# The first RMSNorm of a hybrid decoder step: its squares summed on VectorE alone, its products earlier in TensorE's order

## Chip, cores and metric

The kernel runs on one core of a Trainium2 chip. The metric is the device time in microseconds of one execution. Several executions are timed and the median is given; one further execution is recorded by the hardware profiler, and all rows of "the profile" come from that one.

The engines are called as in the profile: PE (TensorE; PEld are its weight loads), DVE (VectorE), ACT (ScalarE), POOL (GpSimd) and SP (SyncE, which here only issues DMA transfers). Each engine takes its instructions in the order of its own queue.

## What is computed

The reference is one inference step of a decoder layer: a group of 1024 prompt tokens and a group of 8 x 4 sample tokens share the weights. Cut to what matters here:

```python
def rmsnorm(x, g):
    var = jnp.mean(x * x, axis=-1, keepdims=True)
    return x * lax.rsqrt(var + EPS) * g

def reference(x_prompt, x_sample, mem_prompt, ..., norm_mix, w_in, ..., w_mem_k, w_mem_v, ...):
    p_mem_k = einsum('bmd,lde->lbme', mem_prompt, w_mem_k)      # (256 memory rows, 1024) @ (1024, 1024)
    p_mem_v = einsum('bmd,lde->lbme', mem_prompt, w_mem_v)
    ...
    u = rmsnorm(h, norm_mix)                                    # h is x at first
    proj = einsum('bld,de->ble', u, w_in)
    ...                                                         # mixers, cross-attention, SwiGLU, final norm
```

Everything is float32. Each float32 operand of a matrix product is split into a high and a low part (`hi`, `lo`), and three products hi*hi, hi*lo and lo*hi are summed, so each product costs three matmuls and each operand one ACT copy (the high part) and one subtraction on DVE or POOL (the low part).

## The kernel before

Activations lie feature by token: `x` is 8 tiles of 128 features by T = 1056 tokens (1024 prompt, 32 sample). The kernel begins with a stage that does two things side by side.

*The memory keys and values.* There are 16 weight strips `w_kv[i]` of 128 x 1024 floats (512 KB each). Strips 0 to 7 are the key strips; strip m gives one output tile `pk` by 24 matmuls (lines 153 to 155), which ACT copies to `kt` and writes out. Strips 8 to 15 are the value strips; each adds 12 matmuls (lines 376 to 378) to the four sums `pv` that stay in PSUM through all eight. `issue(i)` loads strip i into one of six raw buffers; `split(i)` makes `kvh` on ACT (line 275) and `kvl` on DVE (line 276).

*The norm of x.* It needs the sum of squares over all 1024 features of every token. Tile k of x is loaded by SP (line 339), squared by ACT (`sq`, line 225; the first one straight into `acc`, line 223) and added to `acc` (line 226). `rstd_all` then gives the reciprocal roots: `token_rstd` multiplies `acc` with ones in 9 small products on PE (`pv`, line 252), DVE and ACT form the root (`newton`, lines 184 to 189), and one step later PE spreads the result over all partitions by transposes (`pb`, line 323), which ACT copies to `rb0` (line 324). `norm_x(c)` scales the x tiles of token chunk c (352 tokens) by `rb0` and the gain (line 331, DVE) and splits them into `uh` (line 332, ACT) and `ul` (line 333, DVE and POOL in turn).

`beside(i)` ties the two together. It is called once ahead of the products of each strip i from 0 to 15, and issues in this order: the load of x tile i - 1, the load of weight strip i + 5, the split of strip i + 1, and the square of one x tile, two strips behind the load of that tile. In the kernel before, POOL adds the squares of tiles 1 to 4 and DVE those of tiles 5 to 7.

*The order of the work.* PE's and SP's instructions run in the order in which the program writes them. In this first stage ACT's and DVE's do too (`kv_order`), among themselves; instructions written after `kv_order.close()`, such as those of `norm_x`, are placed by a scheduler and may go in between where it finds a gap. `spawn(gen)` starts a generator that yields a number of steps to wait; `tick()`, called after each value strip's products (and twice per key strip), runs what has come due. So where `rstd_all` is spawned in `beside` settles behind which strip's products PE takes the products of line 252, and one strip later the transposes.

*After the stage.* The first thing PE does with the normalised x is `dt_unit(0)` (line 428, 16 products for a chunk, read from `uh` and `ul`), then the first mixer strip on chunk 0 (lines 153 to 155), then the same for chunks 1 and 2. `dt_unit` takes a PSUM tile of the three that the value sums held.

SP loads the constants `cst` (gains and biases), the masks `msk` (with the identity that the transposes read) and `wdt` in three transfers, issued in this kernel at strip 11, behind all other loads of the stage. The tiles of x, `uh`, `ul`, the raw weights, the split weights, `acc`, `sq` and others share 28 buffers of one size (`slot`).

Of the kernel before, what the change touches and what calls it, by code (L numbers as in the profile page):

```python
# [23 lines left out]
KD = DM // P  # L24
# [35 lines left out]
def hybrid_step(ctx, tc, xT, memT, consts_d, masks_d, wbd_d, poolw_d, spool_d, w_kv, w_xbc, w_dt, w_lg, w_pool, w_z, h0_d,  # L60
                w_out1, w_out2, w_q, kc_d, vc_d, w_o, w_gu, w_down,
                yT, ktT, vN, smallo, pssd, sssd):
    nc = tc.nc
# [11 lines left out]
    def nm(s):  # L75
        cnt[0] += 1
        return f"{s}{cnt[0]}"

    def slot(dt=F32, name="s"):
        return sl.tile([P, T], dt, tag="slot", name=nm(name))  # L80
# [5 lines left out]
    def spawn(gen):  # L86
        step(gen)
# [6 lines left out]
    def tick():  # L94
        now[0] += 1
        while queue and queue[0][0] <= now[0]:
            step(heapq.heappop(queue)[2])
# [123 lines left out]
    def square_into(acc, src, first, tmp, eng=nc.gpsimd):  # L221
        if first:
            nc.scalar.activation(acc, src, AF.Square)
        else:
            nc.scalar.activation(tmp, src, AF.Square)
            eng.tensor_tensor(acc, acc, tmp, op=OP.add)
# [40 lines left out]
    def issue(i, a=0, b=DM):  # L267
        nc.sync.dma_start(raws[i % 6][:, a:b], w_kv[i][:, a:b])

    def split(i, part=(0, DM)):  # L270
        if part[0] == 0:
            kvw[i] = slot(F32R, "kvh")[:, :DM], slot(F32R, "kvl")[:, :DM]
        b = slice(*part)
        hi, lo = (t[:, b] for t in kvw[i])
        nc.scalar.activation(hi, raws[i % 6][:, b], AF.Copy)
        nc.vector.tensor_tensor(lo, raws[i % 6][:, b], hi.bitcast(F32), op=OP.subtract)
# [32 lines left out]
    acc = slot(name="acc")  # L309
    xs = []  # L310

    def rstd_all():
        yield 0
        t9 = tp.tile([P, 27], F32, tag="cy", name="t9", bufs=5, padded_shape=[P, CY])
        r, v, q = t9[:, :9], t9[:, 9:18], t9[:, 18:]
        token_rstd(acc, r, v, q)
        yield 1
        for a in range(0, 9, 4):
            pb = smps(name="pb")
            n = min(T - a * P, 512)  # L320
            for t in range(a, min(a + 4, 9)):
                w = min(P, T - t * P)
                nc.tensor.transpose(pb[:, (t - a) * P:(t - a) * P + w], r[:w, t:t + 1].to_broadcast([w, P]), ident[:w, :w])
            nc.scalar.activation(rb0[:, a * P:a * P + n], pb[:, :n], AF.Copy)
# [10 lines left out]
    def beside(i):  # L335

        if 0 <= i - 1 < KD:
            x = slot(name="x")
            nc.sync.dma_start(x, xT[(i - 1) * P:(i - 1 + 1) * P, :])
            xs.append(x)  # L340
        if i + 5 < 16:
            issue(i + 5)
        if i + 1 < 16:
            split(i + 1)
        k = i - 1 - 2
        if 0 <= k < KD:
            square_into(acc, xs[k], k == 0, slot(name="sq") if k else None, nc.vector if k > 4 else nc.gpsimd)
        if k == KD - 1 + 2:
            spawn(rstd_all())

    for m in range(8):
        beside(m)
        pk = ps.tile([P, 256], F32, tag="mm", name=nm("pk"), bufs=3)
        unit(pk, kvw[m], mpairs, slice(0, 256), KD)
        kt = tp.tile([P, 256], F32, tag="cy", name=nm("kt"), bufs=5, padded_shape=[P, CY])
        nc.scalar.activation(kt, pk, AF.Copy)
        nc.scalar.dma_start(ktT[m * P:(m + 1) * P, :], kt)
# [6 lines left out]
    pv = [ps.tile([P, 512], F32, tag="mm", name=nm("pvv"), bufs=3) for _ in range(3)] + [smps(name="pvv")]  # L364
    for k in range(KD):
        beside(8 + k)
        if k == 3:
            nc.sync.dma_start(cst, consts_d)
            nc.sync.dma_start(msk, masks_d)
            nc.sync.dma_start(wdt, w_dt)  # L370
        whi, wlo = kvw[8 + k]
        for i in range(2):
            for j in range(2):
                a, e = slice(i * P, (i + 1) * P), slice(j * 512, (j + 1) * 512)
                hi, lo = mpairs[k]
                nc.tensor.matmul(pv[2 * i + j], hi[:, a], whi[:, e], start=k == 0, stop=False)
                nc.tensor.matmul(pv[2 * i + j], lo[:, a], whi[:, e], start=False, stop=False)
                nc.tensor.matmul(pv[2 * i + j], hi[:, a], wlo[:, e], start=False, stop=k == KD - 1)
        tick()
# [539 lines left out]
    acc = rp.tile([P, T], F32, tag="acc", name="acc_mem", bufs=1)  # L919
# [369 lines left out]
    for c in range(2):  # L1289
        for m in range(8):  # L1290
# [7 lines left out]
            if m:  # L1298
                sq = fp.tile([P, 2, HB], F32, tag="sq2", name=nm("sq"), bufs=2)
# [136 lines left out]
    def beside():  # L1436
# [3 lines left out]
        yield from sums(1, 2)  # L1440

    spawn(beside())
    g2 = [slot2(F32, "tm") for _ in range(2)]
    w4 = [batches.pop(0)[0] for _ in range(4)]
# [125 lines left out]
    if True:  # L1570
# [26 lines left out]
        for a, b in LAST:  # L1597
            for m in range(8):
# [4 lines left out]
                sq = fp.tile([P, b - a], F32, tag="ar", name=nm("sq"), bufs=4, padded_shape=[P, T])  # L1603
# [123 lines left out]
```

## Time and profile before

| | |
|---|---|
| median of 3 executions | 1797.31 us (1793.78 to 1799.6) |
| the profiled execution, its own time | 1793.21 us |
| its span, first to last instruction | 1791.4 us |
| PE busy | 1721.7 us (96%) |
| PE weight loads busy | 1669.3 us (93%) |
| DVE, ACT, POOL busy | 1160.0, 778.4, 644.0 us |
| granted PE clock | 0.992 |

How to read it: busy times are sums over the whole span, and an engine that is busy much of the time need not be the one waited for. A row of a timeline gives the start in us, the duration, the engine, the line of the program, the operation, the tiles (written <- read), the shape and a count, and in brackets how long the engine had been idle and what ended that. A row of waits gives who waited for whom, the total in us, how often, and the longest. Matmul ends are modelled and matmuls overlap, so starts of weight loads are the surer sign of a PE that waits.

### The profile page before, as it was taken

What the parts mean: (1) busy time and instruction counts of PE and PEld (TensorE: products, weight loads), DVE (VectorE), ACT (ScalarE), POOL (GpSimd) and SP (SyncE); (2) the same over time, 40 slices, a digit from 0 to 9 for tenths busy, and PEclk for the clock granted to TensorE, in tenths of its full rate; (3) what the DMA queues carried; (4) which work ended last, traced back from release to release, by engine and by line L of the source; (5) the groups of instructions that cost most, each with busy time, mean ns of one, the idle gap of its engine ahead of it and who ended that gap; (6) DMA issues with size and microseconds to landing.
All of it is one profiled execution on the core that took longest, in us unless ns stands there. A gap on an engine that the chain in (4) does not pass through costs nothing.

```text
span 1791.4 us, 31915 instructions
## 1 busy us (share of the span) xinstructions
PE 1721.7 (96%) x12307; PEld 1669.3 (93%) x12307; DVE 1160.0 (65%) x2141; ACT 778.4 (43%) x1525; POOL 644.0 (36%) x650
## 2 busy tenths in 40 slices
PE   8899989999999999999999989999999999899997
PEld 7798988888999999999999979999999999899896
DVE  5888998788753534445567469655555556786855
ACT  6544444467744313345565255222322224353344
POOL 2423456665342322212222143443343332211435
PEclk9999999999999999999999999999999999999999
DMA  9111222242230522234345240223332224543322
GB/s 349 62 49 66 65 70 88 96 142 69 86 126 20 201 105 75 79 115 129 117 138 180 89 145 8 105 100 112 108 108 90 96 91 159 208 165 108 122 72 97
DMA packets 106504, 197.52 MB, mean 110 GB/s; under 512 B 15344, under 2 KB 33392, under 8 KB 106352
## 3 DMA queue, kind: packets, MB, share of 16 engines
q1 hardware_dynamic: 94832, 173.54, 28.9%
q10 hardware_dynamic: 11520, 21.94, 3.3%
q8 instruction: 97, 1.59, 0.4%
q14 instruction: 55, 0.45, 0.1%
HBM read 151.54 MB, written 43.89 MB: 109 GB/s over the span
## 4 chain that ended last, share of the span: by engine, by line
PE 76%; DVE 12%; issue 4%; POOL 3%; DMA 2%; ACT 2%; SPq 0%; ACTq 0%; DVEq 0%; POOLq 0%
PE mm L153 11%; PE mm L155 11%; PE mm L154 11%; PE st L1326 10%; PE st L1327 10%; PE st L1328 10%; DVE cy L504 2%; PE poa L1083 1%; PE pss L1065 1%; DVE xd L1372 1%; POOL seg L576 1%; DVE x L331 1%; PE st L1454 1%; PE st L1456 1%; PE st L1455 1%
## 5 line engine op out<-in xcount | busy, mean ns | idle before, releaser
L153 PE MATMUL mm<-uh,whi 128*128 128x352 f32 x960 | 319.8, 333 | 0.0
L1326 PE MATMUL st<-x,whi 128*128 128x264 f32 x1120 | 318.8, 285 | 0.9 <-ACT tm L1506 0.9
L1327 PE MATMUL st<-x,whi 128*128 128x264 f32 x1120 | 318.1, 284 | 0.0
L1328 PE MATMUL st<-x,wlo 128*128 128x264 f32 x1120 | 318.0, 284 | 0.0
L155 PE MATMUL mm<-uh,wlo 128*128 128x352 f32 x960 | 310.1, 323 | 0.0
L154 PE MATMUL mm<-ul,whi 128*128 128x352 f32 x960 | 309.9, 323 | 0.0
L1326 PEld LDWEIGHTS st<-x,whi 128*128 128x128 f32 x1120 | 210.7, 188 | 1.2 <-ACT tm L1506 1.1
L1328 PEld LDWEIGHTS st<-x,wlo 128*128 128x128 f32 x1120 | 210.7, 188 | 0.0
L1327 PEld LDWEIGHTS st<-x,whi 128*128 128x128 f32 x1120 | 210.6, 188 | 0.0
L153 PEld LDWEIGHTS mm<-uh,whi 128*128 128x128 f32 x960 | 181.1, 189 | 4.3 <-issue 1.9
L154 PEld LDWEIGHTS mm<-ul,whi 128*128 128x128 f32 x960 | 181.5, 189 | 2.5
L155 PEld LDWEIGHTS mm<-uh,wlo 128*128 128x128 f32 x960 | 180.8, 188 | 0.0
L1326 PE MATMUL st<-xd,whi 128*128 128x264 f32 x504 | 144.7, 287 | 13.1 <-ACT w L1552 6.5
L1327 PE MATMUL st<-xd,whi 128*128 128x264 f32 x504 | 144.2, 286 | 0.0
L1328 PE MATMUL st<-xd,wlo 128*128 128x264 f32 x504 | 143.9, 285 | 0.0
L1259 ACT ACTIVATE whi<-as 128x512 fp32r<-128x512 f32 (+1 forms) x128 | 74.7, 584 | 140.9 <-PE st L1327 96.3
L1244 POOL TENSOR_TENSOR as<-ar 128x512 f32<-128x512 f32 (+1 forms) x32 | 53.3, 1665 | 205.9 <-DVE wlo L1260 174.3
L1259 ACT ACTIVATE whi<-ar 128x512 fp32r<-128x512 f32 (+1 forms) x104 | 60.8, 587 | 148.2 <-PE st L1327 84.7
L123 ACT ACTIVATE whi<-wraw 128x512 fp32r<-128x512 f32 x128 | 77.9, 626 | 104.1 <-PE mm L154 74.1
L1326 PEld LDWEIGHTS st<-xd,whi 128*128 128x128 f32 x504 | 95.8, 190 | 14.6 <-ACT w L1552 6.7
L958 POOL TENSOR_TENSOR kvlo<-kvraw,kvhi 128x512 fp32r<-128x512 f32 x32 | 41.4, 1295 | 162.2 <-ACT kvhi L957 129.9
L1328 PEld LDWEIGHTS st<-xd,wlo 128*128 128x128 f32 x504 | 95.7, 190 | 0.0
(461 smaller groups left out, 4483.2 us busy)
## 6 DMA issues: line engine op xcount, KB each, us to landing
ar<-w_gu SPq DMA_DIRECT2D x88, 256.0 KB, 4.0
hid_dram<-tm SPq DMA_DIRECT2D x71, 264.0 KB, 2.2
xd<-hid_dram SPq DMA_DIRECT2D x63, 264.0 KB, 4.8
ar<-w_down SPq DMA_DIRECT2D x48, 192.0 KB, 3.2
h_dram<-h ACTq DMA_DIRECT2D x16, 528.0 KB, 2.9
h<-h_dram SPq DMA_DIRECT2D x16, 528.0 KB, 6.5
seg<-acs_dram SPq DMA_DIRECT2D x32, 256.0 KB, 3.8
wraw<-w_out SPq DMA_DIRECT2D x32, 256.0 KB, 3.5
```

Of the source, the lines that this page charges most:

```text
L123: nc.scalar.activation(hi[:, a:b], raw, AF.Copy)
L153: nc.tensor.matmul(out, whi[:, a:b], xh[:, cols], start=k == 0, stop=False)
L154: nc.tensor.matmul(out, whi[:, a:b], xl[:, cols], start=False, stop=False)
L155: nc.tensor.matmul(out, wlo[:, a:b], xh[:, cols], start=False, stop=k == kk - 1)
L331: nc.vector.scalar_tensor_tensor(x, x, cc("gmix", k), rb0[:, ch(c)], op0=OP.mult, op1=OP.mult)
L504: nc.vector.scalar_tensor_tensor(y[:, :n], raw[:, j:j + n], w[j], y[:, :n], op0=OP.mult, op1=OP.add)
L958: eng.tensor_tensor(lo, src, hi.bitcast(F32), op=OP.subtract)
L1244: nc.gpsimd.tensor_tensor(s1, a21, a22, op=OP.add)
L1259: nc.scalar.activation(hi[:, a], src, AF.Copy)
L1326: nc.tensor.matmul(out, whi[:, a:b], xh, start=begins and k == 0, stop=False, skip_group_check=True)
L1327: nc.tensor.matmul(out, whi[:, a:b], xl, start=False, stop=False, skip_group_check=True)
L1328: nc.tensor.matmul(out, wlo[:, a:b], xh, start=False, stop=k == kk - 1, skip_group_check=True)
```

## The change

```diff
@@ def beside(i):
             issue(i + 5)
         if i + 1 < 16:
             split(i + 1)
-        k = i - 1 - 2
+        k = i - 1 - 1
         if 0 <= k < KD:
-            square_into(acc, xs[k], k == 0, slot(name="sq") if k else None, nc.vector if k > 4 else nc.gpsimd)
-        if k == KD - 1 + 2:
+            square_into(acc, xs[k], k == 0, slot(name="sq") if k else None, nc.vector)
+        if k == KD - 1:
             spawn(rstd_all())
@@ the value strips
     for k in range(KD):
         beside(8 + k)
-        if k == 3:
+        if k == 0:
             nc.sync.dma_start(cst, consts_d)
             nc.sync.dma_start(msk, masks_d)
             nc.sync.dma_start(wdt, w_dt)
```

All seven additions to `acc` run on DVE. Tile k is squared at i = k + 2 instead of k + 3, one strip behind its load. `rstd_all` is spawned at i = 9 (with the last square) instead of i = 12, so in PE's order its products stand behind strip 9's instead of strip 12's, and the transposes behind strip 10's instead of strip 13's. The three constant loads are issued at strip 8, behind weight strip 13 and ahead of strips 14 and 15, instead of at strip 11.

## The prediction

> **What bounds the kernel now.** I read the page's engine shares first, then its chain, then a table of stretches around the first norm, then what PE's weight loads waited for there, and last the timelines of the engines that feed them.
>
> ```profile
> PE 1721.7 (96%) x12307; PEld 1669.3 (93%) x12307; DVE 1160.0 (65%) x2141; ACT 778.4 (43%) x1525; POOL 644.0 (36%) x650
> ...
> PE 76%; DVE 12%; issue 4%; POOL 3%; DMA 2%; ACT 2%; SPq 0%; ACTq 0%; DVEq 0%; POOLq 0%
> ```
>
> TensorE carries 76% of the chain, so time can only be won where PE waits. The table of stretches (stretch, length, then busy us and count of PE, PEld, DVE, ACT, POOL, clock, DMA share, GB/s) shows such a place before 90 us:
>
> ```profile
> 22.70:35.40 12.70, 11.99 (x97) 11.38 (x95) 6.16 (x4) 9.68 (x12) 9.18 (x4) 1.00 1.04 413
> ...
> 41.73:50.10 8.37, 8.37 (x38) 6.76 (x37) 6.82 (x12) 4.64 (x7) 3.88 (x3) 1.00 0.61 205
> 50.10:52.25 2.15, 2.15 (x21) 2.08 (x19) 0.00 (x0) 0.00 (x0) 0.00 (x0) 1.00 0.55 192
> ...
> 63.60:86.50 22.90, 17.71 (x98) 15.23 (x97) 22.86 (x34) 13.37 (x29) 12.01 (x12) 1.00 0.13 47
> 90.00:130.00 40.00, 40.00 (x253) 39.31 (x252) 34.68 (x99) 17.98 (x43) 9.10 (x24) 1.00 0.13 42
> ```
>
> From 63.6 to 86.5 DVE is busy 22.86 of 22.90 us and PE is not: there the normalisation (L331 to L333) bounds. From 90 on PE is full. Between 50.1 and 52.25, while PE makes the norm's products, DVE and ACT do nothing at all. What the weight loads waited for, first from 19 to 42 us, then from 56 to 90:
>
> ```profile
> PEld pk L155 <- DVE kvl L276: 1.7, 4, 0.5
> PEld pvv L378 <- DVE kvl L276: 1.3, 2, 0.8
> ```
> ```profile
> PEld mm L428 <- DVE ul L333: 4.3, 5, 2.0
> PEld mm L428 <- POOL ul L333: 2.0, 2, 1.0
> PEld mm L428 <- issue: 1.3, 1, 1.3
> PEld pvv L378 <- DVE kvl L276: 1.8, 1, 1.8
> ```
>
> So some 3.0 us are lost behind the split weights before 42 us, 1.8 at the last V strip, 1.3 at the first dt product, and 6.3 behind the normalised x. That is all the change can reach.
>
> **Part 1: the squares on DVE, one strip earlier.** Four additions leave POOL, four join DVE. DVE and POOL:
>
> ```profile
> 24.61 1.23 DVE L276 TENSOR_TENSOR kvl<-kvw,kvh 128x1024 fp32r<-128x1024 f32 x1 [2.02 <-DMA ktT<-kt]
> 27.45 1.79 DVE L276 TENSOR_TENSOR kvl<-kvw,kvh 128x1024 fp32r<-128x1024 f32 x1 [1.62 <-DMA ktT<-kt]
> ...
> 37.57 1.90 DVE L276 TENSOR_TENSOR kvl<-kvw,kvh 128x1024 fp32r<-128x1024 f32 x1 [1.51 <-ACT kvh L275]
> ...
> 44.00 1.25 DVE L226 TENSOR_TENSOR acc<-acc,sq 128x1056 f32<-128x1056 f32 x1
> ```
> ```profile
> 25.64 2.53 POOL L226 TENSOR_TENSOR acc<-acc,sq 128x1056 f32<-128x1056 f32 x1 [24.37 <-ACT sq L225]
> ```
>
> The added cost is 4 x 1.25 = 5.0 us of DVE. It hides: DVE is busy 6.16 of 12.70 us in 22.7 to 35.4, and each addition follows a kvl with 1.5 to 2 us of idle time after it. Were that cover gone, the 5.0 us would stand ahead of a kvl. The saving: the kvl subtraction takes 1.23 us with POOL idle and 1.79 to 1.90 (first and last of four) while POOL adds, about 0.6 each. The PE waits above are mostly these.
>
> The Trainium skill ("SBUF — State Buffer", Who interferes with whom) says that the second of two such instructions blocks until the first has ended; by it the kvl of 27.45 would wait until 28.17 and take 1.95. The trace has 1.79, a little less than a full lock; by the lock the four would save 0.15 us each more, which the ACT bound below takes away again.
>
> What is late next is ACT, whose queue holds kvh, the square, the copy kt and its DMA issue in each strip:
>
> ```profile
> 22.70 0.38 ACT L356 ACTIVATE kt<-pk 128x256 f32<-128x256 f32 x1 [0.39 <-PE pk L155]
> ...
> 25.56 0.38 ACT L356 ACTIVATE kt<-pk 128x256 f32<-128x256 f32 x1
> ...
> 35.60 0.39 ACT L356 ACTIVATE kt<-pk 128x256 f32<-128x256 f32 x1 [0.50 <-PE pk L155]
> ...
> 39.37 1.07 ACT L225 ACTIVATE sq<-x 128x1056 f32<-128x1056 f32 x1
> ```
>
> Back to back, one strip costs ACT 25.56 - 22.70 = 2.86 us. Four strips from 22.70 end at 34.1 instead of 35.6: 1.5 us won. V strip 9 ended at 41.73 (three strips of 12 products later, at 50.10, the norm's products began); with its 0.8 us wait gone too it ends at 39.4. Without POOL's additions nothing else changes for POOL: it has no other work before 45 us that anyone waits for.
>
> **Part 2: the norm's products after V strip 9 instead of 12.** The spawn moves from i = 12 to i = 9 (in the code three strips). Before, acc was ready at 44.00 + 1.25 = 45.25 and PE came for it only at 50.1. Now x is the limit. Its loads, on SP and by DMA (last figure: us to landing), with the constants behind them:
>
> ```profile
> 31.59 0.33 SPq L339 DMA_DIRECT2D x<-xT  x1
> 32.67 7.15 SPq L268 DMA_DIRECT2D kvw<-w_kv  x3
> 39.88 0.42 SPq L368 DMA_DIRECT2D cst<-consts_d  x1
> ```
> ```profile
> x<-xT SPq DMA_DIRECT2D x1, 528.0 KB, 6.8
> ```
>
> The last x is issued at 31.59 and lands at 38.4; the DMA share there is 1.04, so I take it as no earlier. Square 1.07, add 1.25: acc at 40.7. PE arrives at 39.4 and waits 1.3 us, a new wait with all of V strip 10 behind it. The products end at 40.7 + 2.15 = 42.9, against 52.25: 9.4 us earlier, of which 8.4 (the three strips now behind them) is order and 1.0 is won. If ACT keeps the old 39.37 for this square, acc comes at 41.7 and the shift is 8.4.
>
> PE's weight loads and DVE after the products:
>
> ```profile
> 50.10 2.13 PEld L252 LDWEIGHTS pv<-ones,acc 128*128 128x128 f32 x18
> ...
> 56.53 0.19 PEld L376 LDWEIGHTS pvv<-kvh,mhi 128*128 128x128 f32 x1
> ...
> 61.40 0.19 PEld L378 LDWEIGHTS pvv<-kvl,mhi 128*128 128x128 f32 x1 [1.77 <-DVE kvl L276]
> ```
> ```profile
> 55.21 1.23 DVE L276 TENSOR_TENSOR kvl<-kvw,kvh 128x1024 fp32r<-128x1024 f32 x1
> 56.67 2.79 DVE L331 SCALAR_TENSOR_TENSOR x<-x,cst,rbc 128x352 f32<-128x352 f32 x4 [0.23 <-ACT rbc L324]
> 59.38 1.97 DVE L276 TENSOR_TENSOR kvl<-kvw,kvh 128x1024 fp32r<-128x1024 f32 x1
> ...
> 84.46 0.51 DVE L333 TENSOR_TENSOR ul<-x,uh 128x352 fp32r<-128x352 f32 x1
> ```
>
> The spawned step brings more than PE's 18 products: a small POOL memset, seven short DVE instructions, a square root with its table on ACT, then nine transposes on PE and three copies on ACT. Behind the square root, which waits for the products, stands the split of V strip 11 on ACT and DVE, as that of strip 14 did; its kvl ended at 55.21 + 1.23 = 56.44, 4.2 us after the products' end, so kvl 11 ends at 47.1. Strip 13 and the transposes took 56.53 - 52.25 = 4.3 us, so strip 11 starts at 47.2 and needs that kvl with its third product, at 47.7: hidden, with 0.6 us to spare.
>
> L331 starts 56.67 - 52.25 = 4.4 us after the products; I keep that distance, so it starts at 47.3. It writes x in place and needs no new buffer, while PE still has V strips 11 to 15 to do. DVE then owes what it owed before (it ran without a pause from 56.67 to 84.97) plus kvl of strips 12 to 14, 3 x 1.23 = 3.7: the last ul comes at 84.97 - 9.4 + 3.7 = 79.3, 5.7 us earlier. With acc at 41.7 it is 4.7. POOL's ul subtractions slow L331, as two rows show:
>
> ```profile
> L331 DVE SCALAR_TENSOR_TENSOR x<-x,cst,rbc x24: 571/574/1302, 56.7 to 83.3; 128x352 f32<-128x352 f32 x24
> ```
> ```profile
> 56.53:86.50 29.97, 18.23 (x24) 1.00 0.12 44
> ```
>
> 24 x 0.574 = 13.8, so contention costs 4.5 us. The uh and ul buffers come free only as weight buffers do, so some of the first L331 will meet no POOL work. The bounds are 0 and 4.5; I take 0.5, near the lower end, since the four L331 in the first row above took 0.70 each.
>
> The other bound is PE: 1.0 won at the products plus the 6.3 behind ul is 7.3; with the 1.8 at the kvl gone too, 9.1. I leave the 1.8 in, at strip 12 now: there too L331 is ready one kvh earlier than the kvl. The 1.3 at L428 I leave as well: dt's PSUM tile has to wait for a V result to be copied out. The two limits are 4.7 to 10.2 on DVE and 7.3 to 9.1 on PE, and the smaller counts: 5.7 + 0.5 = 6.2 us, between 4.7 and 9.1.
>
> **Part 3: the constants.** The old place, with each load's landing:
>
> ```profile
> cst<-consts_d SPq DMA_DIRECT2D x1, 328.0 KB, 5.5
> ```
> ```profile
> msk<-masks_d SPq DMA_DIRECT2D x1, 228.0 KB, 5.7
> ```
>
> Three issues of some 0.45 us move past two kvw loads on SP; those wait for their buffers anyhow (x3 took 7.15 us), so SP has the room. With 64 KB for wdt (128 x 128 floats) they move 620 KB, at 413 GB/s 1.5 us, by which kvw 14 and 15 land later; PE starts strip 14 at about 55 (47.2 and three strips of 2.8), so they have 10 us in hand. If that cover were gone, it would cost 1.5. At the old place cst would land at 45.4 and the masks, whose identity the transposes read at about 46, at 46.1: the move is worth 0.1 and I count nothing.
>
> **After 90 us** PE and DVE both stand 6 us earlier, and I carry that to the end. The order on ACT, DVE and POOL isn't fixed by hand after this stage, so I add 2 us of spread both ways.
>
> **Sum.** The profiled execution took 1793.21 us (span 1791.4); 6.2 less gives 1787.0. The median of the runs is 1797.31, 4.1 above that execution, so the forecast is 1797.3 - 6.2 = 1791.1, and its own range 1788 to 1793.
>
> **Rivals.** *Both limits give way* (chance 0.12): POOL meets few L331 and the kvl wait goes; 9.1 us, 1788.2. The free DVE time in 41 to 62 speaks for it, the 0.70 us of the first L331 against.
>
> *Half is given back* (0.22): the wait at the products grows, or DVE puts two or three L331 ahead of each of the kvl 12 to 15. Each such kvl costs PE what the one at 61.40 cost, 1.77 us; three more are 5.3, leaving 0.9: 1796.4. For it: that row. Against it: after strip 12 each kvl is ready early, because its load landed long before.
>
> *The clock falls* (0.02, counted within the 0.22): acc comes only at 43, PE waits 3.4 us, 2.1 more than in the sum, and the V strip after it, at half rate, takes 2.8 longer: 1796. The longest gap behind ul was 2.0 us and the clock column stays at 1.00 through it, so the trace neither shows nor excludes it. The Trainium skill ("TensorE: Matmul & The Clock Gate", Why this matters for your kernels) states the rule: gaps of about 3 us between bursts put the array back to half clock.
>
> *Slower* (0.11): the whole block of 24 L331 stands ahead of kvl 12 in DVE's queue, and V strip 12 behind it. kvl 12 is due at about 50.5 (strip 11 starts at 47.2, takes 2.8, and 0.5 into strip 12). With n of them it ends at 47.3 + 0.76 n + 1.23; for 24 that is 66.8, a wait of 16.3 where 9.1 can be won: 7.2 slower, 1804.5. It decides from n = 15. For it: four already stood ahead of a kvl. Against: an old kvl never waited for more.
>
> **How the numbers follow.** The forecast has 0.55; three quarters of it lie beyond 0.3% (5.4 us, about what a measurement here can tell from no change). Faster: 0.41 + 0.12 = 0.53. Same: 0.14 + 0.22 = 0.36. Slower: 0.11. The range 1786 to 1798 takes in the first three but for their tails and leaves out the last.
>
> **What the new profile would show.** kvl at 1.23 all through; acc adds on DVE only, the last ending near 40.7; PE's 18 pv loads near 41 after a wait of about 1 us; L331 from 47; waits at L428 down from 7.6 to about 2 us; the last ul near 79; PE full from then. A pv start after 43, or a kvl of strips 12 to 15 that PE waits over 2 us for, makes the prediction wrong; so do new waits after 130 us.

## The result, and the profile after

| | before | after |
|---|---|---|
| median | 1795.55 us (6 runs, 1792.25 to 1799.6) | 1805.22 us (6 runs, 1802.68 to 1807.9) |
| profiled execution, its span | 1793.21, 1791.4 us | 1806.24, 1804.5 us |
| granted PE clock | 0.992 | 0.986 |

The ratio after to before is 1.0053, 95% interval [1.0035, 1.0072]: the change makes the kernel slower by about 9.7 us. The forecast was 6.2 us faster, and its range ended at 1798. The two profiled executions lie 13.0 us apart, since that of before was 2.3 us below its median and that of after 1.0 above; the rows below account for these two.

What PE's weight loads waited for from 40 to 112 us of after (who, for whom: total us, times, longest); nothing else there reaches half a microsecond:

```profile
PEld mm L155 <- DVE wlo L124: 13.5, 1, 13.5
PEld mm L428 <- POOL ul L333: 2.6, 1, 2.6
PEld pv L252 <- DVE acc L226: 1.3, 1, 1.3
PEld pvv L378 <- DVE kvl L276: 0.4, 1, 0.4
```

The 1.8 us behind a `kvl`, which the forecast left in, have shrunk to 0.4. The waits behind the normalised x once the dt products have begun (6.3 us in all before) are gone, but not because `ul` came earlier: the last one of all ends at 86.16 us in after (the row at 84.91 below) and ended at 86.25, on POOL, before. PE came for them later still, because a wait that no part of the forecast had stood in front: 13.5 us for `wlo`, the low part of the first mixer strip's weights. The same weight loads as a timeline of after:

```profile
43.03 2.67 PEld L252 LDWEIGHTS pv<-ones,acc 128*128 128x128 f32 x18 [1.32 <-DVE acc L226]
...
68.68 0.19 PEld L428 LDWEIGHTS mm<-uh,dpad 128*128 128x128 f32 x1 [2.58 <-POOL ul L333]
...
85.04 0.29 PEld L155 LDWEIGHTS mm<-uh,wlo 128*128 128x128 f32 x1 [13.47 <-DVE wlo L124]
```

The program (`split_into`) splits each weight strip in two halves of 512 columns. ACT makes the high part `whi` of both, DVE the low part `wlo` of the first half and POOL that of the second. It always splits one strip ahead of the one asked for, so two `wlo` on DVE belong here: the first halves of the first and of the second mixer strip. Where they were in the kernel before:

```profile
47.88 0.68 DVE L124 TENSOR_TENSOR wlo<-wraw,whi 128x512 fp32r<-128x512 f32 x1
52.43 0.17 DVE L254 TENSOR_SCALAR t<-pv 128x8 f32<-128x8 f32 x1 [3.87 <-PE pv L252]
...
52.97 0.69 DVE L124 TENSOR_TENSOR wlo<-wraw,whi 128x512 fp32r<-128x512 f32 x1 [0.33 <-issue]
```

and in after:

```profile
41.73 1.25 DVE L226 TENSOR_TENSOR acc<-acc,sq 128x1056 f32<-128x1056 f32 x1
...
45.88 0.17 DVE L254 TENSOR_SCALAR t<-pv 128x8 f32<-128x8 f32 x1 [2.54 <-issue]
...
52.33 2.07 DVE L331 SCALAR_TENSOR_TENSOR x<-x,cst,rbc 128x352 f32<-128x352 f32 x4 [2.44 <-ACT rbc L324]
...
81.58 1.74 DVE L331 SCALAR_TENSOR_TENSOR x<-x,cst,rbc 128x352 f32<-128x352 f32 x2
83.24 1.75 DVE L124 TENSOR_TENSOR wlo<-wraw,whi 128x512 fp32r<-128x512 f32 x1
84.91 1.25 DVE L333 TENSOR_TENSOR ul<-x,uh 128x352 fp32r<-128x352 f32 x1
```

Before, both of DVE's `wlo` ran in the quiet stretch around the norm's products, ahead of the first L331. In after that stretch comes at 43.2 to 45.9, and the high part from which `wlo` is taken isn't there yet. ACT, before (first row) and after:

```profile
46.88 1.95 ACT L123 ACTIVATE whi<-wraw 128x512 fp32r<-128x512 f32 x3 [1.26 <-DMA wraw<-w_xbc]
```
```profile
51.70 1.18 ACT L324 ACTIVATE rbc<-pb 128x512 f32<-128x512 f32 x3 [3.07 <-PE pb L323]
52.75 1.07 ACT L275 ACTIVATE kvh<-kvw 128x1024 fp32r<-128x1024 f32 x1
53.70 1.16 ACT L123 ACTIVATE whi<-wraw 128x512 fp32r<-128x512 f32 x2
```

The split of the first mixer strip is written behind the whole normalisation and placed by the scheduler. In after it put the copies `whi` behind `rbc` on ACT; by 54 us L331 is ready and stands earlier in the program, and all 24 of it go ahead of the first `wlo` on DVE, although its high part was there at about 54.3. POOL made its half of the same strip from 54.94 to 56.70. PE works on what it has until 71.57 us and stands still for 13.47, until 85.04.

The granted clock shows a second loss. Stretches of after (length, then busy us of PE, PEld, DVE, ACT, POOL, clock, DMA share, GB/s):

```profile
44.00:44.20 0.20, 0.20 (x4) 0.20 (x3) 0.00 (x0) 0.00 (x0) 0.00 (x0) 0.93 0.87 338
44.20:44.40 0.20, 0.20 (x3) 0.20 (x3) 0.00 (x0) 0.00 (x0) 0.00 (x0) 0.50 0.80 256
...
50.80:51.00 0.20, 0.20 (x1) 0.00 (x1) 0.00 (x0) 0.00 (x0) 0.00 (x0) 0.50 0.00 0
51.00:51.20 0.20, 0.20 (x3) 0.20 (x2) 0.00 (x0) 0.00 (x0) 0.00 (x0) 1.00 0.00 0
...
74.80:75.00 0.20, 0.00 (x0) 0.00 (x0) 0.20 (x2) 0.20 (x2) 0.03 (x1) 0.73 0.00 0
88.40:88.60 0.20, 0.20 (x2) 0.20 (x2) 0.00 (x0) 0.00 (x0) 0.00 (x0) 0.64 0.86 307
...
63.60:86.50 22.90, 7.54 (x36) 6.39 (x35) 22.90 (x33) 10.32 (x22) 12.84 (x11) 0.75 0.16 58
90.00:130.00 40.00, 40.00 (x253) 39.34 (x252) 29.48 (x87) 16.94 (x38) 6.41 (x20) 1.00 0.07 21
```

From 44.17 to 51.00 PE ran at half clock: the products took 2.67 instead of 2.13 us, and V strip 10 some 4.9 instead of 2.8, together 2.6 us more. The clock falls again during the long wait and stays low behind it, from 74.89 to 88.54. From 63.6 to 86.5 PE worked 7.54 us where it had worked 17.71, while DVE was never idle. From 90 on PE is full again.

The account runs from the end of V strip 9, which comes at about 41.7 us in both executions, to the first `pdt` product, behind the last work that waits on this stage. The group of `pdt`, before and after (count, least/median/greatest ns, first and last start):

```profile
L440 PE MATMUL pdt<-msk,dtT x8: 221/222/260, 92.5 to 93.0; 48*128 48x48 f32 x8
```
```profile
L440 PE MATMUL pdt<-msk,dtT x8: 221/222/257, 105.2 to 105.6; 48*128 48x48 f32 x8
```

It comes 12.7 us later. The terms:

| what PE lost or won from 41.7 us to `pdt` | us |
|---|---|
| wait at the norm's products | +1.3 |
| half clock at the products and in V strip 10 | +2.6 |
| wait for a `kvl`, 0.4 instead of 1.8 | -1.4 |
| wait at the first dt product, 2.6 instead of 1.3 | +1.3 |
| wait for `wlo` | +13.5 |
| half clock behind it (13 weight loads, 0.29 apart instead of 0.16) | +1.7 |
| waits behind `ul`, 0 instead of 6.3 | -6.3 |
| waits at the transposes, 0.4 instead of 0.7 | -0.3 |
| sum | +12.4 |

Less the 6.3 us of waits that it hid, the late `wlo` cost 8.9 of this. The span grew by 13.1, so all of it is carried to the end.

### The profile page after: what moved, and what is told of

It is laid out like the page before. It is cut to its first block, busy times and chain, and to the rows that moved or that the text cites. A ratio compares the mean times of both kernels' runs of the same rounds, so it can differ in the third digit from the quotient of the medians.

```text
span 1804.5 us, 31904 instructions
## 1 busy us (share of the span) xinstructions
PE 1725.8 (96%) x12307; PEld 1675.9 (93%) x12307; DVE 1166.4 (65%) x2145; ACT 777.4 (43%) x1525; POOL 623.6 (35%) x646
## 5 line engine op out<-in xcount | busy, mean ns | idle before, releaser
L155 PEld LDWEIGHTS mm<-uh,wlo 128*128 128x128 f32 x960 | 181.3, 189 | 13.5 <-DVE wlo L124 13.5
L1326 PE MATMUL st<-xd,whi 128*128 128x264 f32 x504 | 145.3, 288 | 12.4 <-ACT w L1552 7.1
L123 ACT ACTIVATE whi<-wraw 128x512 fp32r<-128x512 f32 x128 | 77.9, 626 | 105.2 <-PE mm L154 77.3
```

The lines of the kernel that those rows point to most:

```text
L123: nc.scalar.activation(hi[:, a:b], raw, AF.Copy)
L155: nc.tensor.matmul(out, wlo[:, a:b], xh[:, cols], start=False, stop=k == kk - 1)
L1326: nc.tensor.matmul(out, whi[:, a:b], xh, start=begins and k == 0, stop=False, skip_group_check=True)
```

## The experiments

Each kernel was timed against the kernel before on the same chip; the ratios are to that. The time at which `pdt` starts shows what the stage alone gained or lost, but only roughly: the second copy `kt`, up to which all these kernels have the same work, comes anywhere from 16.05 us (e4) to 18.07 (after), 16.63 in before. A table further down counts `pdt` from there. The expectations' theory A: the late `wlo` costs the time. B: the wait at the products and the half clock cost it. In the second group, where `wlo` is in time, D says that ACT's wait for a raw buffer eats the forecast's gain, and E that `uh` and `ul` have no free buffers before PE ends the value strips.

### Is it the late low half?

**e1: the change, with the split of the first mixer strip written ahead of `norm_x(0)`**, which only changes its place in the order.

```diff
     kv_order.close()
+    w_first = next(weights)
     norm_x(0)
...
-            w = next(weights)
+            w = w_first if m == 8 else next(weights)
```

> The changed kernel with one edit: the first mixer weights (strips 0 and 1) are taken in the program ahead of norm_x(0), so that the scheduler may place their low parts on DVE ahead of the normalisation. Theory A (the two halves of the first strip's wlo, line 124, stand behind all 24 of line 331 in DVE's queue, and PE waits 13.5 us for them): that wait goes, the last dt product comes near 84.5 to 85 instead of 98.96, the time is 1790 to 1795 where the changed kernel has 1805. Theory B (the loss is made by the wait at the norm's products and the half clock after it, and the normalised x is late whatever wlo does): another wait of about the same size takes its place, 1800 to 1805. The half clock behind the products stays in both.

1796.63 us, ratio 1.0007 [0.9992, 1.0021], pdt at 94.7. The loss is gone, and so is every wait for `wlo`; the wait at the products and the half clock (44.66 to 48.07) are still there. A holds, though the time lies 1.6 us above its range: no gain has come instead. Why, in ACT's, DVE's and PE's rows of this kernel:

```profile
61.25 0.63 ACT L123 ACTIVATE whi<-wraw 128x512 fp32r<-128x512 f32 x1 [5.70 <-DMA wraw<-w_xbc]
```
```profile
62.31 1.33 DVE L333 TENSOR_TENSOR ul<-x,uh 128x352 fp32r<-128x352 f32 x1 [4.82 <-ACT uh L332]
```
```profile
PEld mm L429 <- issue: 7.3, 1, 7.3
```

A `whi` on ACT waited 5.7 us for a raw buffer, and the `uh` that stand behind it in ACT's queue ran from 61.79 us on, right after it. (What the expectation calls the two halves of the first strip's `wlo` are, as said above, the first halves of two strips.)

**e2: the change, but with the products one strip later** (`k == KD - 1` becomes `k == KD`: strip 10), so that PE finds `acc` ready.

> The changed kernel with the norm's products one strip later (spawn at i = 10). PE should no longer wait for acc (ready near 43, PE there near 44.5) and the clock should stay at 1.00 behind the products: 1.3 + 0.5 + 2.1 us less before the end of the value strips. Theory A: wlo still stands behind the normalisation, whose start moves by only 1 to 2 us, so 1802 to 1805. Theory B: the 3.9 us and the waits that follow go, 1796 to 1801.

1805.45 us, ratio 1.0061 [1.0048, 1.0074], pdt at 101.8. In the waits and the weight loads of this kernel the products have lost their wait, and the clock stays at 1.00 behind them, but `wlo` is as late as ever:

```profile
PEld mm L155 <- DVE wlo L124: 14.9, 1, 14.9
```
```profile
43.10 2.13 PEld L252 LDWEIGHTS pv<-ones,acc 128*128 128x128 f32 x18
```

The stage ended 3.4 us earlier than in after (1.9 counted from the second `kt`) and the whole took no less: 4.2 us of the span's growth over before arose behind `pdt`. So what B names costs the stage 1.9 to 3.4 us, and is not the main cause of the loss.

**e3: the change, but with the products behind strip 12 as before** (`k == KD + 2`).

> Squares on DVE one strip behind the load, and the constants at strip 8, but the norm's products behind strip 12 as in the kernel before. Theory A: wlo finds its old gap on DVE while PE makes the products, no new wait: 1793 to 1797, the kvl subtractions at 1.23 us winning up to 2 us. Theory C (the squares on DVE or the constants ahead of the last two weight strips cost the time): 1800 to 1805.

1793.33 us, ratio 0.9991 [0.998, 1.0001], pdt at 91.5. `wlo` ran at 47.13 and 51.59, ahead of the first L331 at 55.68. With the products' place alone undone, the loss is gone.

**e5: the kernel before with only the split of that strip held back behind all of `norm_x`** (`kv_order.close()` and `w_first = next(weights)` moved there; this holds the norm itself to the order of the program too).

> The kernel before (squares two strips behind, products behind strip 12, constants at strip 11) with one thing forced: the split of the first mixer strip is written, and kept in order, behind all of the normalisation on ACT and DVE. Theory A says that this alone does what the change did: PE waits some 10 to 14 us for wlo at the first mixer strip, 1804 to 1810. Theory B (the change's earlier products are needed for the loss): 1795 to 1799.

1817.27 us, ratio 1.0128 [1.0108, 1.0148], pdt at 114.8: the sign is as expected, the time above the range, because the high half is held back too and PE waits for that:

```profile
PEld mm L153 <- ACT whi L123: 18.8, 1, 18.8
PEld mm L429 <- issue: 7.7, 1, 7.7
```

So holding this split back behind the normalisation is enough, without the change, to make PE wait for it longer than it did in after (18.8 us against 13.5). The other wait, 7.7 at L429 where it was 1.3 before, may come from the norm's being held in order; the two were not tried apart, and so the whole loss of this run can't be put down to the split.

### With the low half in time, where is the gain?

**e4: e1 with the products at strip 10.**

> Both edits: the first mixer weights ahead of norm_x(0) and the norm's products behind strip 10. Theory A: no wlo wait, no wait for acc, no half clock; line 331 starts near 51 instead of 56.7, two kvl more stand among it, so the last dt product comes 2.5 to 4 us before that of the kernel before: 1791 to 1794. Theory B: as the second run, 1796 to 1801.

1796.14 us, ratio 1.0005 [0.9991, 1.0019], pdt at 92.6. Wait and half clock at the products are gone, and still nothing is won. The time is the one that B expected, but neither of B's two losses is there. POOL's rows, one `wlo` of its own among DVE's run of `kvl`, `wlo` and L331, and one later:

```profile
52.05 5.86 POOL L124 TENSOR_TENSOR wlo<-wraw,whi 128x512 fp32r<-128x512 f32 x1 [11.00 <-ACT whi L123]
61.25 1.27 POOL L124 TENSOR_TENSOR wlo<-wraw,whi 128x512 fp32r<-128x512 f32 x1 [3.34 <-ACT whi L123]
```

The first took 5.86 us and held its raw buffer as long; ACT's next `whi` waited 5.6 us for one, with `uh` behind it. It started 2.6 us after POOL's subtraction ended, in e4 (57.91 and 60.54) as in e1 (58.64 and 61.25).

**e6 and e7: e4 and e1 with a fourth raw buffer** (`bufs=3` becomes `bufs=4` for `wraw`), so that ACT needn't wait.

> The fourth run's kernel (first mixer weights ahead, products behind strip 10) with a fourth raw weight buffer. There ACT stood 5.6 us at the fourth whi half, because its load waited for a buffer that a 5.86 us POOL subtraction held, and all uh stood behind it in ACT's queue. Theory D (this head-of-line wait eats the gain): it goes, line 332 runs from about 54.5 on, the last dt product comes at 80 to 82 instead of 85.1, 1788 to 1792 beside 1796 for the fourth run. Theory E (uh and ul have no free buffers before PE ends the value strips, so the normalisation can't go ahead anyhow): within 1 us of the fourth run, 1794 to 1797.

> The same fourth raw buffer with the products behind strip 9, as in the change, and the first mixer weights ahead of norm_x(0). The wait for acc and the half clock behind the products stay (about 3.9 us of PE). Theory D: DVE is the bound and starts line 331 at about the same time as with strip 10, so the time is that of the run with strip 10 or up to 2 us more, 1788 to 1794. Theory E: 1794 to 1798.

e6: 1795.64 us, ratio 1.0006 [0.9991, 1.0021], pdt at 91.4. e7: 1797.64, 1.0015 [1.0002, 1.0028], pdt at 93.5. ACT's wait is gone in both, and `pdt` comes 1.2 us earlier than in e4 and e1 (2.6 and 2.0 counted from the second `kt`). So the buffer did cost the stage something, as D says; that the whole is no shorter is lost behind `pdt`, where these two spans grew by 3.3 and 4.1. E's mechanism isn't there: four `uh` of e6 ran from 56.41 us on, while PE was busy with the value strips until about 62. DVE now runs without a pause to the last `ul` and sets the pace. e6, DVE and POOL:

```profile
50.86 2.07 DVE L331 SCALAR_TENSOR_TENSOR x<-x,cst,rbc 128x352 f32<-128x352 f32 x4 [0.29 <-ACT rbc L324]
52.85 1.22 DVE L276 TENSOR_TENSOR kvl<-kvw,kvh 128x1024 fp32r<-128x1024 f32 x1
53.99 0.69 DVE L124 TENSOR_TENSOR wlo<-wraw,whi 128x512 fp32r<-128x512 f32 x1
...
56.33 1.22 DVE L276 TENSOR_TENSOR kvl<-kvw,kvh 128x1024 fp32r<-128x1024 f32 x1
...
58.10 3.15 DVE L331 SCALAR_TENSOR_TENSOR x<-x,cst,rbc 128x352 f32<-128x352 f32 x2
...
83.43 0.51 DVE L333 TENSOR_TENSOR ul<-x,uh 128x352 fp32r<-128x352 f32 x1
```
```profile
53.47 7.40 POOL L124 TENSOR_TENSOR wlo<-wraw,whi 128x512 fp32r<-128x512 f32 x2 [11.01 <-ACT whi L123]
```

L331 starts 5.8 us earlier than before (56.67), and DVE's last `ul` comes only 1.0 us earlier (84.46), so 4.8 us are used up in between. Counted from start to start: three `kvl` (52.85, 54.59, 56.33) take 3.4, where the single one before (59.38, slowed beside POOL) took 1.9, 1.5 more; two `wlo` (53.99, 55.73) that the gap used to hide take 1.2; the small subtraction for `dpad`, free of POOL here, takes 0.8 less; and L331 and `ul` together take 27.1 us instead of 24.3, 2.8 more. For POOL's two `wlo` had run ahead of the first `ul` before (at 48.27 and 55.77), and now they meet L331 and `ul`: the two L331 at 58.10 took 3.15 us, where the next two before (62.65) took 1.07. That was the forecast's gain.

**e8: e6 with the value copies `vn` written ahead of `norm_x(0)`**, so that PSUM comes free earlier for the first dt product.

> As the run with strip 10 and four raw buffers, and the copies of the value sums out of PSUM are written ahead of norm_x(0), so that ACT and DVE make them as soon as PE ends and the first dt product gets its PSUM tile. In the fourth run PE waited 3.2 us there. If that wait bounds the stage: 1 to 2 us less than without it. If DVE's ul at the end of the stage bounds it, no difference.

1798.29 us, ratio 1.001 [0.9996, 1.0025], pdt at 94.0: no gain, and `pdt` 2.6 us later than in e6. PE found other things late, in the same place:

```profile
PEld mm L429 <- DVE ul L333: 3.6, 1, 3.6
PEld mm L429 <- issue: 2.4, 1, 2.4
PEld mm L429 <- ACT uh L332: 1.3, 1, 1.3
PEld mm L429 <- POOL ul L333: 1.2, 1, 1.2
```

**e12: e6 with all 24 L331 written ahead of the first `uh` and `ul`**, to see whether POOL's `ul` beside L331 is what DVE loses.

> As e6_w1_10_raw4 (products at strip 10, first mixer strip's weights written ahead of the normalisation, four raw buffers), with all 24 scalings (L331) written ahead of the first uh and ul. If DVE's work of about 33 us (24 scalings, 12 ul, 4 kvl, 2 low halves) is the bound and POOL's ul slow the scalings, the scalings now run at 0.57 to 0.65 us instead of up to 1.6, the last ul comes 2 to 4 us earlier than in e6 and pdt at 88 to 90; but the first dt product then waits for all of chunk 0's uh and ul until after 66. If the first products of dt set the rest, pdt comes at 93 to 96 and the time is 1797 to 1801.

1801.68 us, ratio 1.0029 [1.0017, 1.0042], pdt at 97.4. This kernel's line numbers are 2 to 5 higher (L333 is the scaling, L337 the `ul`):

```profile
57.63 12.07 DVE L333 SCALAR_TENSOR_TENSOR x<-x,cst,rbc 128x352 f32<-128x352 f32 x20
...
75.44 6.93 DVE L337 TENSOR_TENSOR ul<-x,uh 128x352 fp32r<-128x352 f32 x6 [0.16 <-ACT uh L336]
```
```profile
PEld mm L433 <- issue: 9.0, 1, 9.0
```

The scalings, ahead of all `ul`, took 0.60 us each, and six `ul` then took 1.15 each instead of 0.51: now these pay for POOL's `ul` beside them. DVE's last `ul` comes 1.6 us earlier than in e6 (82.37 against 83.94), where 2 to 4 were expected, and PE waits 9.0 us for the first chunk, so that `pdt` and the time lie a little above even the worse of the two outcomes expected.

### The parts alone

**e9: the squares alone** (all on DVE, one strip behind the load; products at strip 12, constants at strip 11). **e10: the constants alone. e11: the whole change with the products behind strip 11.**

> The kernel before with the squares alone changed (all on DVE, one strip behind the load); products at strip 12, constants at strip 11. Theory A (only the place of the first mixer strip's low half in DVE's queue costs time, and here it keeps its old place, about 47 and 52): no change, 1793 to 1797; kvl 1.23 us in all strips, strip 9 still ends at 41.5 to 41.9, since with kvl faster the next thing that PE waits for is no earlier; PE at pdt 91.5 to 92.6. Rival (the forecast's part 1: the waits behind kvl are lost time that comes back): strip 9 ends at 39.4 to 40.2, pdt at 90.2 to 91, 1793 to 1794. Rival (the five us of additions on DVE cost something): 1798 or more.

> The kernel before with the constants alone moved to strip 8. By the forecast's part 3 they cost nothing: 1794 to 1797, pdt at 92.2 to 92.9, x7 lands no later than 38.5, kvl 12 to 15 waits unchanged (1.8 in all). Rival (the 620 KB delay weight strips 14 and 15): up to 1.5 us more, PE waits behind kvl 14 or 15.

> The whole change, but the products behind strip 11 instead of 9: one strip earlier than before. Theory A: the low half of the first mixer strip comes at 45 to 53, in the gap beside the products, no wait behind it over 1 us, and the time is at most that of the kernel before: 1791 to 1796. If only the earlier norm counted (forecast), the stage would end 2.8 us earlier less one kvl, 1.2: pdt 90.5 to 91.5. If the earlier products cost time by themselves whatever becomes of the low half, it is slower than before by a third of the change's loss, 1799 or more.

e9: 1793.51 us, ratio 0.9983 [0.9968, 0.9998], pdt at 91.3. e10: 1794.42, 0.999 [0.9976, 1.0004], pdt at 92.8. e11: 1794.98, 0.9996 [0.9983, 1.0009], pdt at 92.3. The constants cost nothing that can be told from zero. The squares on DVE win 1.2 us at `pdt` (1.6 counted from the second `kt`), and e9 has the lowest ratio of all; its interval only just leaves out no change. Waits behind `kvl` up to 45 us in e9, against 1.7 and 1.3 before:

```profile
PEld pk L155 <- DVE kvl L276: 0.6, 3, 0.2
PEld pvv L378 <- DVE kvl L276: 0.5, 1, 0.5
```

In e11 the split keeps its place by itself (DVE's `wlo` at 53.34, ahead of the first L331 at 55.04), and the products come at 47.09, 3.0 us earlier than before; yet the last wait behind `ul` ends at 86.14 against 86.31 before and 85.16 in e9. Counted from the second `kt` that is 68.3, 69.7 and 68.1: all that e11 wins, e9 has too. What was earlier is filled, as in e6: one `kvl` more stands among the L331, and beside them a `wlo` on POOL that took 3.24 us.

The stage by itself, and what the span of the profiled execution gained or lost over before behind `pdt` (us):

| kernel | `pdt` | `pdt` counted from the second `kt` | span behind `pdt` |
|---|---|---|---|
| before | 92.5 | 75.9 | |
| after | 105.2 | 87.1 | +0.4 |
| e1, first strip ahead, products at strip 9 | 94.7 | 78.0 | -0.4 |
| e2, products at 10 | 101.8 | 85.2 | +4.2 |
| e3, products at 12 | 91.5 | 74.3 | -1.4 |
| e4, first strip ahead, products at 10 | 92.6 | 76.6 | +0.4 |
| e5, before with the split held back | 114.8 | 98.4 | +0.3 |
| e6, e4 with four buffers | 91.4 | 74.0 | +3.3 |
| e7, e1 with four buffers | 93.5 | 76.0 | +4.1 |
| e8, e6 with `vn` ahead | 94.0 | 76.3 | +6.3 |
| e9, squares alone | 91.3 | 74.2 | +2.2 |
| e10, constants alone | 92.8 | 75.7 | +0.4 |
| e11, products at 11 | 92.3 | 74.5 | +1.9 |
| e12, e6 with all L331 ahead | 97.4 | 79.9 | +2.6 |

By the third column the squares on DVE shorten the stage by 1.6 us (e9, and e3, which has the constants moved too), and the earlier products add at most 0.3 to that (e6).

What stays open is the last column: why behind `pdt` the span grew by 3.3 to 6.3 us in e2, e6, e7 and e8 and by 1.9 to 2.6 in e9, e11 and e12. These are single executions, and the order on ACT, DVE and POOL later on differs between the kernels; which piece of it costs time wasn't tried.

## Why the prediction was wrong

*Part 1, the squares.* Right that POOL's additions stretch `kvl` (1.23 us everywhere in after) and that the additions on DVE are hidden. Wrong in size: the strips were not ACT-bound at 2.86 us. The copies `kt` of after, second and last of eight, and the second and third of before:

```profile
18.07 0.39 ACT L356 ACTIVATE kt<-pk 128x256 f32<-128x256 f32 x1 [2.39 <-PE pk L155]
...
36.33 0.39 ACT L356 ACTIVATE kt<-pk 128x256 f32<-128x256 f32 x1 [0.39 <-PE pk L155]
```
```profile
16.63 0.39 ACT L356 ACTIVATE kt<-pk 128x256 f32<-128x256 f32 x1 [1.93 <-PE pk L155]
...
19.46 0.38 ACT L356 ACTIVATE kt<-pk 128x256 f32<-128x256 f32 x1 [0.97 <-PE pk L155]
```

Six strips in 18.26 us are 3.04 each (before, 16.63 to 35.60, 3.16): 0.7 us won by the last copy, not 1.5. The 2.86 was one of the short strips, which come in turn with long ones: before, from 19.46 to 22.70, ahead of POOL's first addition at 25.64, a strip took 3.24, and in after ACT waits some 0.4 us for PE in every second one. With the `kvl` waits of the first value strips 1.4 us were won by the end of V strip 9. It ended all the same where it had (about 41.7), not at 39.4, because in this execution the second `kt` came 1.4 later.

*Part 2, the products.* The wait of 1.3 us came as forecast, but by luck: `acc` ended at 42.98 instead of 40.7, and PE came 2.3 us late too. x was not the limit: the load of its last tile was issued at 31.33, and none of the last five took over 8.1 us, but ACT squared it only at 40.08, behind another square and a split, and DVE's addition stood behind a `kvl` until 41.73. That `pv` (43.03) fell past the 43 named as the mark of an error is chance as well; in e1, whose second `kt` came at 16.75, it started at 41.67. The rival of the falling clock named an `acc` at 43, which came, and a wait of 3.4 us, which was 1.3. The clock fell even so, and it cost 2.6, near that rival's 2.8. The block of 24 L331 did stand ahead of something, but not of `kvl` 12: the longest wait for a `kvl` was 0.4 us. So the rival "slower" was right about the engine and wrong about what was blocked, and that its time fits (1804.5 forecast, 1805.2 measured) is luck.

*The step that failed* is in Part 2: "DVE then owes what it owed before ... plus kvl of strips 12 to 14". It listed three `kvl` and left out DVE's two `wlo`, which had run in the idle gap at 47.88 and 52.97 that the change was to close, and PE's side of the sum counted waits for x alone. Put in, the two lower the gain by 1.2 to 1.4 us if they keep their place ahead of L331, and where the scheduler put them behind it the first of them made PE wait 13.5. The forecast read "DVE and ACT do nothing at all" from the stretch 50.10 to 52.25 as waste; the stretch just around it held another consumer's work. The contention credit of 0.5 us was also of the wrong sign: L331 and `ul` together took 1.2 us more in after than before, and 2.8 more in e6, where POOL's `wlo` stood beside L331. The start of L331 was too early in the sum as well: it came at 52.33, not 47.3, because `acc` was 2.3 late, the products took 0.5 longer and V strip 10, at half clock, held the transposes back by another 2.2. Together these put DVE's last `ul` at 86.16, not near 79; before, it ended at 84.97, and POOL's last at 86.25. So even with `wlo` in time the normalisation of this execution would have ended no earlier than before. And the 1.3 at the first dt product became 2.6: POOL's `ul` ended at 68.39, but the copy `vn` on ACT, behind `uh` in its queue, at 68.62, and the product started at 68.68. That it waited for `vn` is read from these times; before, `vn` ended at 64.80 and the product started at 64.87.

*Part 3 and after 90 us.* Right: the constants cost nothing that shows (e10), and what the stage lost was carried to the end unchanged (12.7 at `pdt`, 13.1 in the span). The 2 us of spread allowed for a later change of order were too few for several of the experiments (3.3 to 6.3 us in e2, e6, e7 and e8).

## What to carry to other kernels

Before closing an engine's idle gap, list every instruction that runs in or next to it, on the other engines too, and ask where each goes when the gap moves: here those that the scheduler places went behind what was ready first and written earlier. An engine that is busy without a pause over a stretch is the bound there only for the work that someone waits for; here one subtraction near the end of DVE's queue, 0.7 us when alone and 1.75 where it stood, cost PE 13.5 us. When work moves earlier, add up what the freed stretch had hidden, with what it costs to run beside the rest, and check that the sum is less than the shift.

## What the chip showed that was not expected

*The clock falls without a long wait.* In after, e1 and e7 PE waited 1.3 us and then ran 18 products of one column in 2.0 to 2.7 us, and the clock fell to 0.50; in the other eleven kernels the same products, without the wait, kept it at 1.00. Which of the two, the wait or the thin products, weighs how much was not tried apart. The changes lie on a grid: in after at 44.17, 51.00, 74.89 and 88.54 us (read from the shares 0.93, 0.73 and 0.64 of the rows above), which lie 2, 7 and 4 steps of 3.41 apart. In e1 half clock lasted 3.41 us (44.66 to 48.07), in e7 6.82 (43.62 to 50.44). The Trainium skill ("TensorE: Matmul & The Clock Gate", Part 1: The HAM clock gate (the "warmup" mystery)) gives a free-running window of 3413 ns, and these traces agree with that step to 0.01 us. Its rule of thumb cited in the prediction, that it is gaps of some 3 us which bring half clock, does not cover this case: 1.3 us of waiting with a run of one-column products behind it did it too.

*POOL starves beside a run of DVE work.* One subtraction of 128 x 512 on POOL took 1.27 us alone and 5.86 in e4 (6.56 in e1) beside `kvl`, `wlo` and L331 back to back, while DVE's two `kvl` beside it in e4 (53.17 and 54.90) took 1.22 each. The Trainium skill ("SBUF — State Buffer", Who interferes with whom) says that such instructions contend and that the order of issue decides who blocks. The rows agree that they contend; but POOL's subtraction, recorded from 52.05 on, held up none of the DVE instructions issued after it until 56 us, so POOL can lose several rounds in a row. The wait then travelled through a raw buffer to ACT and through ACT's queue to PE (7.3 us in e1).
